# A two-layer decoder trunk on one core: matmul operands at the low end of SBUF, the softmax exchange on ScalarE, x loaded first, and a last FFN part of eight tiles

## The chip, the core and the metric

The kernel runs on one core of one Trainium2 chip. A core has TensorE (PE in the profile; its weight loads are shown apart as PEld), VectorE (DVE), ScalarE (ACT), GpSimd (POOL) and SyncE (SP), which here only starts transfers. SP, ACT and POOL each have a DMA queue. On-chip memory is SBUF, 128 partitions of 224 KB, and PSUM, where products are summed. The metric is the device time of one execution, in microseconds (us); lower is better. Before the change the median of 3 runs is 2288.46 us (2286.1 to 2291.06).

## The reference

One sequence of 512 tokens of width 1024, two layers. All in float32.

```python
def reference(x, ...):
    for l in range(2):
        mix = hybrid_mixer(x, rel_bias, w_in[l], b_in[l], w_attn_proj[l], w_ret_proj[l], w_out[l])
        x = layer_norm(ALPHA * x + mix, ln1_g[l], ln1_b[l])
        x = layer_norm(ALPHA * x + swiglu(x, w_ffn_gate[l], w_ffn_up[l], w_ffn_down[l]), ln2_g[l], ln2_b[l])
    return x

def hybrid_mixer(...):
    z = x @ w_in + b_in                    # split: q,k,v of attention (18 heads of 64); q,k (4 x 256), v, gate (4 x 512)
                                           # of retention; two gates of 1024
    # attention: 3 groups of 6 heads, (window, dilation) = (128,1), (512,4), (2048,16); T5 relative bias;
    # the groups' outputs are summed with weights softmax(log of their softmax denominators)
    # retention: sum over m <= n of gamma^(n-m) (rot(q_n) . rot(k_m)) v_m, group norm, times silu(gate)
    merged = sigmoid(gate_a) * (y_attn @ w_attn_proj) + sigmoid(gate_b) * (y_ret @ w_ret_proj)
    return merged @ w_out

def swiglu(x, w_gate, w_up, w_down):       # inner width 2816 = 22 tiles of 128
    return (silu(x @ w_gate) * (x @ w_up)) @ w_down
```

## The kernel before

Every large product is made of three: each float32 operand is split into a rounded high part (ACT, `CAST`) and the rest (DVE, `TENSOR_TENSOR`), and high by high, high by low and low by high are summed in PSUM. The helper `hilo` makes the two parts, `mm3` issues the three products, all at line L78. The split weights are `whi` and `wlo` (4 buffers each), the split x is `xh` and `xl`, all of x transposed. Weights come through 8 buffers of 4 KB a partition, named `raw`; SP loads most of them.

A layer runs in stages. First the attention's q and k of the first head pair for two groups (`wstat_halves`, in two halves of 256 tokens, since x arrives token tile by token tile), then of the third group (`wstat`: weights stationary, 512 tokens moving). Then v, in two steps, by a seven-product scheme (`tall`, `ORDER`) that saves one product in eight. It needs sums of weight blocks (`P1`, `P3`): SP loads one block into a `raw` buffer and POOL's queue adds the other to it by an accumulating DMA (`Right.load`, L315). It also needs sums of x blocks (`S1` to `S4`, in `xs`), made by `x_sums` from copies of x named `xc`. The biases of these columns are a row product of `bh` and `ones`.

The attention itself is no stage: its small steps (scores, transposes, products with v) stand in a queue `side`, and `tick`, called after each large product, takes steps from it at the rate that `pace` sets. `nothing` entries only space the steps. There are three head pairs `hp`; a pair's steps run beside the q and k products of the next pair. The first group works in token order, the two dilated groups in an order by residue of 4. So after a pair's scores, `swap` copies its maxima `nm` and sums `ls` into `pk` and brings them through DRAM (`exd`) into token order (`mb`); `weigh` computes the weights of both orders and sends the dilated one back through DRAM into `fa`; `scale` multiplies the outputs `y` by `fa` (L553), `place` transposes them into `yaT`. `swap` stands at the end of a pair's steps, the other four (`tail`) among those of the next pair. The biases of the scores come from `bias_vectors`: a table product (`hot`), then `bias_d`, then `bias_r`, a copy for each of 128 partitions, 2.7 MB, then `load_bias` (L745 to L747) reads slices of it.

After that come retention (`rotary`, `ret_values_gates`, `ret_scores`, `ret_outputs`, with operands `rot`, `vr` and `pj`), the gates (`ya` is the split `yaT`), the projection of retention into `m`, and w_out, whose second half has the tokens as the outer loop (`token_outer`): one token tile's 24 products end, then `residual` and `norm` run on DVE while PE goes on with the next tile. The FFN goes in parts of the 22 inner tiles, `FPARTS`; each part makes its tiles `ht` by gate and up products and then adds its down products to the residual. The last part's second half is again token-outer, and its `norm` ends the layer: in layer 0 the result is transposed into the next layer's `xh` and `xl` (`to_xT`), in layer 1 it is stored.

The order on each engine is set by the Tile framework's scheduler, which also places the waits. Tiles come from pools that open and close with the stages; a pool lies where the ones opened before it end, counted from the low end of SBUF.

Of the kernel before, what the change touches and what calls it, by code (L numbers as in the profile page):

```python
# [49 lines left out]
FPARTS = ((0, 8), (8, 16), (16, 22))  # L50
# [3 lines left out]
def hybrid_kernel(ctx, tc, x, rel_bias, w_in, b_in, w_attn_proj, w_ret_proj, w_out,  # L54
# [20 lines left out]
    dve.memset(mhalf, -0.5)  # L75

# [100 lines left out]
    def x_sums(cp):  # L177

        (a11, a12), (a21, a22) = cp
        t = {}  # L180

        def put(n, v):
            o_ = xs[:, SN.index(n)]
            hilo(v, o_[:, 0], o_[:, 1])

        def tt(o_, a, b, op):
            dve.tensor_tensor(out=o_, in0=a, in1=b, op=op)

        def s1():
            t["s"], t["v"] = view(raw("sch"), 4, 256), view(raw("sch"), 4, 256)  # L190
            tt(t["s"], a21, a22, ALU.subtract)
            put("S1", t["s"])

        def s2():
            tt(t["s"], t["s"], a11, ALU.subtract)
            put("S2", t["s"])

        def s4():
            tt(t["s"], t["s"], a12, ALU.add)
            put("S4", t["s"])  # L200

        def s3():
            tt(t["v"], a11, a21, ALU.subtract)
            put("S3", t["v"])

        return [s1, s2, s4, s3]


    def pair_units(w, c, c2=None):

        out_ = []
        for hf in range(2):
            ks = slice(4 * hf, 4 * hf + 4)
            if c2 is None:
                r = load(w[:, ks, c:c + 256], 4, 256)
            else:
                r = view(raw(), 4, 256)
                v = r.rearrange("p k (q c) -> p k q c", q=2)
                for q, cc in enumerate((c, c2)):
                    nc.sync.dma_start(v[:, :, q], w[:, ks, cc:cc + P])  # L220
            out_.append(unit(r))
        return out_
# [251 lines left out]
    def attention_pair(hp, qk, v, yp, bias, yaT):  # L474
# [48 lines left out]

        def swap():

            exd = drp.tile([S, 4], F32, tag="exd", name="exd", bufs=2)
            pk = sm.tile([P, NI, 4], F32, tag="pk", name="pk", bufs=2)
            pool.tensor_copy(pk[:, :, 0:2], nm[:, 1])
            pool.tensor_copy(pk[:, :, 2:4], ls[:, 1])
            pool.dma_start(exd.rearrange("(l r) c -> l r c", r=4), pk)  # L530
            pool.dma_start(mb, exd.rearrange("(i p) c -> p i c", p=P))

        def weigh():
            exd2 = drp.tile([S, 2], F32, tag="exd2", name="exd2", bufs=2)
# [12 lines left out]
            pool.dma_start(exd2.rearrange("(i p) c -> p i c", p=P), wb)  # L547
            pool.dma_start(fa[:, 1], exd2.rearrange("(l r) c -> l r c", r=4))
            dve.tensor_tensor(out=fa[:, 0], in0=ea[:, 0], in1=wa, op=ALU.mult)

# [26 lines left out]
        tail = [weigh, lambda: (scale(0), scale(1)), lambda: place(0), lambda: place(1)]  # L577
# [15 lines left out]
    def layer(ly, cp):  # L593
# [9 lines left out]
        yap = lay.enter_context(tc.tile_pool(name="yap", bufs=1))  # L603
        yaT = yap.tile([P, NG, S], F32, name="yaT")
        csp = lay.enter_context(tc.tile_pool(name="csp", bufs=1))
        opp = lay.enter_context(tc.tile_pool(name="opp", bufs=9))
# [52 lines left out]
        with tc.tile_pool(name="attn", bufs=1) as ap_, tc.tile_pool(name="attw", bufs=4) as aw:  # L659
# [5 lines left out]
            def qk_units(hp, g):  # L665
                c = g * GW + hp * P
                return pair_units(w_l, C_QA + c, C_KA + c)
# [9 lines left out]
            if ly == 0:  # L677
                x0 = [slot("x0", F32) for _ in range(NI)]
                cp = [[slot("xc", F32).rearrange("p a (b t) -> p (a b) t", b=2) for _ in range(2)] for _ in range(2)]
# [416 lines left out]
```

## Time and profile before

| | us |
|---|---|
| median of 3 runs | 2288.46 (2286.1 to 2291.06) |
| the profiled execution's own time | 2290.13 |
| its span, first to last instruction | 2288.1 |
| PE busy | 2246.7 (98%) |
| DVE busy | 1184.5 (52%) |
| ACT busy | 847.9 (37%) |
| POOL busy | 198.9 (9%) |
| mean granted clock of PE | 0.992 |

The profile gives, for one execution, each instruction's start and end, what it waited for, and the clock that PE was granted (1.00 is full speed). A table by stretch sums these over a part of the span; a timeline row gives start, length, engine, line, operation and tiles, and in brackets the wait ahead of it. In rows of the form `out<-in`, buffer numbers are left out.

### The profile page before, as it was taken

To read this page: it belongs to the slowest core of one execution; us is meant where nothing else is said; L and a number is where in the kernel's file an instruction comes from. 1 tells how busy PE (TensorE), PEld (TensorE's weight loads), DVE (VectorE), ACT (ScalarE), POOL (GpSimd) and SP (SyncE) were. 2 spreads that over 40 slices of the span, in tenths; PEclk is the share of its full clock that TensorE was granted. 3 is DMA by queue.
4 is the path that set the end of the run, shared out by engine and by line. 5 is a ranking of instruction groups with operands and counts; after the bars stand their busy time and mean duration, and the time that the engine had idled before them with its cause. 6 is when DMAs were issued, how large, how long until landed. Compare 5 with 4: busy or idle time off the path is not lost.

```text
span 2288.1 us, 27786 instructions
## 1 busy us (share of the span) xinstructions
PE 2246.7 (98%) x10890; PEld 1848.0 (81%) x10890; DVE 1184.5 (52%) x1793; ACT 847.9 (37%) x1359; POOL 198.9 (9%) x276
## 2 busy tenths in 40 slices
PE   8899999999999999999999999999999999999997
PEld 7877778878888888888889777788888888888886
DVE  5534577776335533333576446777753455333345
ACT  4444545545333132222235445445543232322230
POOL 1310011110000100000031111111000001000001
PEclk9999999999999999999999999999999999999999
DMA  6953265455565233333249332665454752233320
GB/s 168 246 146 84 63 175 134 123 140 152 176 225 184 64 110 94 92 102 101 71 124 252 92 85 65 158 172 134 127 163 144 247 166 65 94 100 101 93 74 37
DMA packets 253875, 294.24 MB, mean 129 GB/s; under 512 B 13981, under 2 KB 192497, under 8 KB 253616
## 3 DMA queue, kind: packets, MB, share of 16 engines
q1 hardware_dynamic: 212640, 234.20, 34.1%
q0 software_dynamic: 22032, 45.69, 8.9%
q10 hardware_dynamic: 19072, 12.59, 1.8%
q8 instruction: 85, 1.39, 0.3%
q14 instruction: 46, 0.38, 0.1%
HBM read 266.63 MB, written 28.53 MB: 129 GB/s over the span
## 4 chain that ended last, share of the span: by engine, by line
PE 76%; issue 18%; DMA 3%; DVE 2%; POOL 1%; ACT 0%; SPq 0%; POOLq 0%; DVEq 0%; ACTq 0%
PE ps L78 68%; PE px L78 6%; DMA raw<-in_w_in 1%; PE px L507 1%; PE px L829 1%; POOL ry L121 1%; DMA fa<-exd 0%; DMA x<-in_x 0%; DVE xtok L922 0%; PE px L166 0%; DMA v_d<-sn 0%; DMA exd<-pk 0%; DVE stats L933 0%; DMA exd<-wb 0%; PE px L558 0%
## 5 line engine op out<-in xcount | busy, mean ns | idle before, releaser
L78 PE MATMUL ps<-xh,whi 128*128 128x512 f32 (+1 forms) x1760 | 676.7, 386 | 3.0 <-ACT xh L89 3.0
L78 PE MATMUL ps<-xl,whi 128*128 128x512 f32 (+1 forms) x1760 | 661.6, 376 | 0.1
L78 PE MATMUL ps<-xh,wlo 128*128 128x512 f32 (+1 forms) x1760 | 661.4, 376 | 0.0
L90 DVE TENSOR_TENSOR wlo<-raw,whi 128x1024 fp32r<-128x1024 f32 (+1 forms) x274 | 332.9, 1216 | 555.9 <-ACT whi L89 555.1
L89 ACT CAST whi<-raw 128x1024 fp32r<-128x1024 f32 (+1 forms) x274 | 285.5, 1044 | 493.0 <-PE ps L78 421.9
L78 PEld LDWEIGHTS ps<-xh,whi 128*128 128x128 f32 x1760 | 332.7, 190 | 66.6 <-issue 6.4
L78 PEld LDWEIGHTS ps<-xh,wlo 128*128 128x128 f32 x1760 | 333.0, 189 | 60.3
L78 PEld LDWEIGHTS ps<-xl,whi 128*128 128x128 f32 x1760 | 333.9, 190 | 53.9 <-DVE xl L90 0.8
L78 PE MATMUL ps<-whi,xs 128*128 128x512 f32 (+1 forms) x768 | 224.4, 366 | 4.1 <-ACT whi L324 4.0
L330 DVE TENSOR_TENSOR wlo<-raw,whi 128x1024 fp32r<-128x1024 f32 (+1 forms) x168 | 178.7, 1065 | 91.6 <-ACT whi L324 91.0
L324 ACT CAST whi<-raw 128x1024 fp32r<-128x1024 f32 (+1 forms) x168 | 154.3, 925 | 126.4 <-PE ps L78 98.6
L78 PE MATMUL ps<-whi,ht 128*128 128x512 f32 x608 | 191.0, 393 | 0.0
L78 PEld LDWEIGHTS ps<-whi,xs 128*128 128x128 f32 x768 | 139.5, 190 | 28.8 <-ACT whi L324 6.6
L121 POOL TENSOR_TENSOR ry<-ve,mhalf 128x1 f32<-128x1 f32 x48 | 44.9, 936 | 1145.8 <-DVE ve L120 1145.8
L78 PE MATMUL ps<-wlo,xs 128*128 128x512 f32 (+1 forms) x384 | 139.5, 363 | 0.6 <-DVE wlo L330 0.6
L78 PEld LDWEIGHTS ps<-whi,ht 128*128 128x128 f32 x608 | 114.2, 188 | 28.4
L78 PE MATMUL ps<-wlo,ht 128*128 128x512 f32 x304 | 121.4, 399 | 0.0
L78 PE MATMUL ps<-whi,xh 128*128 128x512 f32 (+1 forms) x288 | 107.1, 372 | 3.6 <-DVE sn L434 3.6
L78 PE MATMUL ps<-whi,xl 128*128 128x512 f32 (+1 forms) x288 | 103.3, 359 | 0.0
L78 PE MATMUL ps<-wlo,xh 128*128 128x512 f32 (+1 forms) x288 | 103.2, 358 | 0.0
L315 POOL DMA_DIRECT2D raw<-in_w_in x48 | 59.3, 1263 | 279.0 <-DMA raw<-in_w_in 156.5
L78 PEld LDWEIGHTS ps<-wlo,xs 128*128 128x128 f32 x384 | 73.1, 190 | 10.3 <-DVE wlo L330 1.6
(172 smaller groups left out, 2526.9 us busy)
## 6 DMA issues: line engine op xcount, KB each, us to landing
raw<-in_w_in SPq DMA_DIRECT2D x144, 512.0 KB, 4.2
raw<-in_w_ffn_gate SPq DMA_DIRECT2D x44, 512.0 KB, 3.8
raw<-in_w_ffn_up SPq DMA_DIRECT2D x44, 512.0 KB, 3.8
raw<-in_w_ffn_down SPq DMA_DIRECT2D x44, 512.0 KB, 3.7
raw<-in_w_in SPq DMA_DIRECT2D x72, 256.0 KB, 4.8
raw<-in_w_in POOLq DMA_DIRECT2D x32, 512.0 KB, 7.5
raw<-in_w_ret_proj SPq DMA_DIRECT2D x32, 512.0 KB, 4.3
raw<-in_w_in SPq DMA_DIRECT2D x40, 288.0 KB, 4.8
```

The source lines that it names most:

```text
L78: pe.matmul(ps, lhsT=a, rhs=b, start=start, stop=stop, skip_group_check=True)
L89: act.copy(out=hi, in_=src)
L90: dve.tensor_tensor(out=lo, in0=src, in1=hi.bitcast(F32), op=ALU.subtract)
L121: pool.tensor_tensor(out=y, in0=ve, in1=mhalf, op=ALU.pow)
L315: pool.dma_start(r, self.src({"P1": "B12", "P3": "B22"}[n], u), accum_op=ALU.add)
L324: act.copy(out=h, in_=src)
L330: dve.tensor_tensor(out=l, in0=src, in1=h.bitcast(F32), op=ALU.subtract)
L507: pe.transpose(px[:, (2 + j) * P:(3 + j) * P], s[:, hh, j * P:(j + 1) * P], ident)
L829: pe.transpose(px[:, t * P:(t + 1) * P], ys[i][:, t * P:(t + 1) * P], ident)
```

## The change

It has these parts.

- **Pools.** `raw` and the small tiles `sm` are put at the high end of SBUF (`side="right"`), with `yaT`, cos and sin and the residual. The weight halves `whi`, `wlo` now follow x directly, and the operands of the stages (`opp`, `fo`, `mp`, `ret`, `attn`) follow those. The pools of the stages wait for earlier users tile by tile (`reuse_waits="tile"`) and not for the whole of a closed pool. The copies `xc` take four `raw` buffers.
- **Exchange.** The copies to `pk` and all four DMAs of the exchange move from POOL to ACT, and four tail steps become seven, each at its own place in `side`.
- **Start.** The identity goes to ACT's queue; x tiles 0 and 1 go ahead of all weights on SP, tiles 2 and 3 between the weight loads. The first units are split into their two column halves (`apart`), and `bias_vectors` runs within the first products.
- **x_sums** works in place, in another order of the four sums.
- **FPARTS** has its short part first: six, eight and eight tiles.

The number of products and of weight bytes is unchanged. Where the tiles lie, in KB of a partition as the two programs are built:

| tile | before | after |
|---|---|---|
| xh, xl, xs | 9 to 73 | 9 to 73 |
| raw | 73 to 105 | 188 to 220 |
| whi, wlo | 105 to 137 | 73 to 105 |
| qk, rot, vr, ya | 163 to 199 | 117 to 153 |
| ht | 177 to 221 | 117 to 161 |
| m | 177 to 209 | 117 to 149 |
| pj | 201 to 211 | 155 to 165 |

```diff
-FPARTS = ((0, 8), (8, 16), (16, 22))
+FPARTS = ((0, 6), (6, 14), (14, 22))
...
-    rawp = ctx.enter_context(tc.tile_pool(name="rawp", bufs=8))
     wp = ctx.enter_context(tc.tile_pool(name="wp", bufs=4))
     wk = ctx.enter_context(tc.tile_pool(name="wk", bufs=6))
-    sm = ctx.enter_context(tc.tile_pool(name="sm", bufs=4))
+    sm = ctx.enter_context(tc.tile_pool(name="sm", bufs=4, side="right"))
+    rawp = ctx.enter_context(tc.tile_pool(name="rawp", bufs=8, side="right"))
...
+    def stage(name, bufs=1, side="left"):
+        return tc.tile_pool(name=name, bufs=bufs, side=side, reuse_waits="tile")
...
+    def x_copies():
+        return [[view(raw("xc"), 4, 256) for _ in range(2)] for _ in range(2)]
...
+    def pair_units(w, c, c2=None, apart=False):
...
+            for hf, q in sorted(todo, key=lambda t: t[::-1]) if apart else todo:
+                nc.sync.dma_start(vs[hf][:, :, q * P:(q + 1) * P], w[:, 4 * hf:4 * hf + 4, (c, c2)[q]:(c, c2)[q] + P])
...
         def swap():
...
-            pool.tensor_copy(pk[:, :, 0:2], nm[:, 1])
-            pool.tensor_copy(pk[:, :, 2:4], ls[:, 1])
-            pool.dma_start(exd.rearrange("(l r) c -> l r c", r=4), pk)
-            pool.dma_start(mb, exd.rearrange("(i p) c -> p i c", p=P))
+            act.copy(out=pk[:, :, 0:2], in_=nm[:, 1])
+            act.copy(out=pk[:, :, 2:4], in_=ls[:, 1])
+            act.dma_start(exd.rearrange("(l r) c -> l r c", r=4), pk)
+
+        def swapped():
+            act.dma_start(mb, exd.rearrange("(i p) c -> p i c", p=P))
...
-            pool.dma_start(exd2.rearrange("(i p) c -> p i c", p=P), wb)
-            pool.dma_start(fa[:, 1], exd2.rearrange("(l r) c -> l r c", r=4))
+            act.dma_start(exd2.rearrange("(i p) c -> p i c", p=P), wb)
             dve.tensor_tensor(out=fa[:, 0], in0=ea[:, 0], in1=wa, op=ALU.mult)
+
+        def weighed():
+            act.dma_start(fa[:, 1], exd2.rearrange("(l r) c -> l r c", r=4))
...
-        tail = [weigh, lambda: (scale(0), scale(1)), lambda: place(0), lambda: place(1)]
+        tail = [swapped, weigh, weighed, lambda: scale(0), lambda: place(0), lambda: scale(1), lambda: place(1)]
...
-        yap = lay.enter_context(tc.tile_pool(name="yap", bufs=1))
+        yap = lay.enter_context(stage("yap", side="right"))
...
-        opp = lay.enter_context(tc.tile_pool(name="opp", bufs=9))
+        opp = lay.enter_context(stage("opp", 9))
...
-                nc.sync.dma_start(ident, c_id)
-                for hf in range(2):
-                    nc.sync.dma_start(x0[0][:, hf], x[:P, hf * S:(hf + 1) * S])
+                act.dma_start(ident, c_id)
...
+                load_x(0)
+                load_x(1)
...
-                us0 = []
-                for g in range(2):
-                    us0.append(qk_units(0, g))
-                    for i in ((1,), (2, 3))[g]:
-                        nc.sync.dma_start(x0[i], x[i * P:(i + 1) * P].rearrange("p (a b) -> p a b", a=2))
+                vecs = bias_vectors([aw.tile([P, S], F32, tag="bias", name="hot") for _ in range(NG)])
+                us0 = [qk_units(0, 0, True)]
+                load_x(2)
+                us0.append(qk_units(0, 1))
+                load_x(3)
+                cp = x_copies()
...
-                side.extend(ops[1] + [lambda l_=l_: bias_cols(l_) for l_ in range(DEPTH)] + ops[2] + ops[3])
+                side.extend(ops[1] + [lambda l_=l_: bias_cols(l_) for l_ in range(DEPTH)] + vecs[:3] + ops[2] + vecs[3:] + ops[3])
...
-            if ly == 0:
-                side.extend([nothing] + bias_vectors([aw.tile([P, S], F32, tag="bias", name="hot") for _ in range(NG)]))
-            pace(8 if ly else 16)
+            pace(8)
...
-                for at, f in zip((27, 25, 22, 15), reversed(tail)):
+                for at, f in zip((24, 22, 15, 14, 12, 8, 3), reversed(tail)):
                     ops.insert(at, f)
...
-        fo = fin.enter_context(tc.tile_pool(name="fo", bufs=11))
+        fo = fin.enter_context(stage("fo", 11))
...
-            if last and not final:
-                cp = [[fo.tile([P, 2, S], F32, tag="op", name="xc").rearrange("p a (b t) -> p (a b) t", b=2)
-                       for _ in range(2)] for _ in range(2)]
...
+                if tail and not final:
+                    cp.extend(x_copies())
```

How the order on the engines moves, at three places. SP, the start of the program, before:

```order
L686 DMA ident<-const_id 128x128
L688 DMA x_111<-in_x 128x512 x2
L220 DMA raw<-in_w_in 128x4x128 x4
L695 DMA x_112<-in_x 128x1024
L220 DMA raw<-in_w_in 128x4x128 x4
```

and after:

```order
L689 DMA x_108<-in_x 128x512 x2
L689 DMA x_109<-in_x 128x512 x2
L209 DMA raw<-in_w_in 128x4x128 x4
L689 DMA x_110<-in_x 128x512 x2
L209 DMA raw<-in_w_in 128x4x128 x4
```

The second tile of x has moved ahead of the first four weight loads. POOL's queue around the v products of layer 0, before (`bias_d` and `bias_r` are the bias vectors, L315 the accumulating weight loads, L745 to L747 the bias slices):

```order
L315 DMA raw<-in_w_in 128x2x288 x4
L463 DMA bias_d<-bv 6x383
L463 DMA bias_d<-bv 6x255 x2
L466 DMA bias_r<-bias_d 128x5358
L408 MEMSET rb 33x576
```

and after:

```order
L458 DMA bias_d<-bv 6x383
L458 DMA bias_d<-bv 6x255 x2
L461 DMA bias_r<-bias_d 128x5358
L403 MEMSET rb 33x576
```

The bias vectors now stand ahead of all accumulating loads (L310 in the new numbering), the first of which follows eight bias slices later. The exchange of the second head pair in layer 0, on POOL before (L315 are weight loads of the next stage):

```order
L528 COPY pk<-nm 128x4x2
L529 COPY pk<-ls 128x4x2
L530 DMA exd<-pk 128x16
L315 DMA raw<-in_w_in 128x2x512
L531 DMA mb<-exd 128x4x4
L547 DMA exd_2230<-wb 128x4x2
L548 DMA fa<-exd_2230 128x8
```

and on ACT after (L513 and L503 are copies of the attention's steps, L92 a weight cast):

```order
L525 COPY pk<-nm 128x4x2
L526 COPY pk<-ls 128x4x2
L527 DMA exd<-pk 128x16
L513 COPY y<-px 128x64 x2
L503 COPY sT<-px 128x256 x2
L530 DMA mb<-exd 128x4x4
L513 COPY y<-px 128x64
L539 ACTIVATE ea<-ea 128x16
L513 COPY y<-px 128x64
L545 DMA exd_1590<-wb 128x4x2
L503 COPY sT<-px 128x256 x2
L92 CAST whi<-raw 128x1024
L513 COPY y<-px 128x64 x2
L549 DMA fa<-exd_1590 128x8
```

On DVE after, the place where the result is used (the scores of the third pair are L492):

```order
L553 TENSOR_TENSOR y<-y,fa 128x512
L93 TENSOR_TENSOR wlo<-raw,whi 128x1024
L675 TENSOR_SCALAR qk<-ps,bT 128x512
L553 TENSOR_TENSOR y<-y,fa 128x512
L93 TENSOR_TENSOR wlo<-raw,whi 128x1024
L492 ISA s,nm<-px,bias 128x128
```

The exchange has left POOL and stands on ACT with two to four of ACT's rows between its steps; on DVE the row that waits for `fa` still stands ahead of the scores, as before.

More of the change, by code (lines that the diff above doesn't have):

```diff
@@ L214, in pair_units @@
             if c2 is None:
-                r = load(w[:, ks, c:c + 256], 4, 256)
+                vs.append(load(w[:, ks, c:c + 256], 4, 256))
             else:
[L217 to L221, printed above, removed]
+                vs.append(view(raw(), 4, 256))
+        if c2 is not None:
+            todo = [(hf, q) for hf in range(2) for q in range(2)]
+            for hf, q in sorted(todo, key=lambda t: t[::-1]) if apart else todo:
+                nc.sync.dma_start(vs[hf][:, :, q * P:(q + 1) * P], w[:, 4 * hf:4 * hf + 4, (c, c2)[q]:(c, c2)[q] + P])
+        if not apart:
+            return [unit(v) for v in vs]
+        out_ = [tuple(view(wp.tile([P, 1024], F32R, tag=t, name=t), 4, 256) for t in ("whi", "wlo")) for _ in vs]
+        for q in range(2):
+            for v, (h, l) in zip(vs, out_):
+                cs = slice(q * P, (q + 1) * P)
+                hilo(v[:, :, cs], h[:, :, cs], l[:, :, cs])
         return out_
@@ L777, in layer @@
                 pace(32)
[L778 removed]
+            n = [nothing]
+            side.extend(n * 3 + tail[:1] + n * 4 + tail[1:2] + n * 3 + tail[2:5] + n * 6 + tail[5:6] + n * 2 + tail[6:])
             pace(42)
```

50 lines of the change are left out of this document (18 added, 32 removed).

## The prediction

> **What bounds the kernel now.** I read the page first, for who is busy and whose chain ends last.
>
> ```profile
> span 2288.1 us, 27786 instructions
> PE 2246.7 (98%) x10890; PEld 1848.0 (81%) x10890; DVE 1184.5 (52%) x1793; ACT 847.9 (37%) x1359; POOL 198.9 (9%) x276
> PE 76%; issue 18%; DMA 3%; DVE 2%; POOL 1%; ACT 0%; SPq 0%; POOLq 0%; DVEq 0%; ACTq 0%
> ```
>
> TensorE (PE) is busy 98% of the span, and the chain that ends last is its products. So the time falls in two ways only: products that follow each other faster, or the 41 us (2288.1 − 2246.7) in which PE does nothing, with the slow clock after each pause. I therefore went on with tables by stretch, in which each row gives the stretch and its length, busy time and count of PE, weight loads, DVE, ACT and POOL, then granted clock and DMA share.
>
> **Pace and addresses.** Two stretches in which PE never pauses and the clock is full, the first in the FFN's gate/up products, the second in its down products:
>
> ```profile
> 920.00:1005.00 85.00, 85.00 (x377) 70.41 (x376) 28.20 (x31) 24.84 (x31) 0.00 (x0) 1.00 0.30 93
> 1007.50:1050.50 43.00, 43.00 (x186) 34.62 (x185) 14.27 (x15) 7.93 (x9) 0.00 (x0) 1.00 0.36 103
> ```
>
> A product's record lasts 0.39 us (groups below), so a stretch counts all that start in its length plus 0.39: 85.39/377 = 0.2265 us from start to start, against 43.39/186 = 0.2333. Same shape, same type, full clock in both. The groups, with count, busy time and mean ns of one, tell the operands apart:
>
> ```profile
> L78 PE MATMUL ps<-xl,whi 128*128 128x512 f32 x446 | 173.7, 390 | 0.0
> L78 PE MATMUL ps<-whi,ht 128*128 128x512 f32 x608 | 191.0, 393 | 0.0
> L78 PE MATMUL ps<-wlo,ht 128*128 128x512 f32 x304 | 121.4, 399 | 0.0
> L78 PE MATMUL ps<-xs,m 128*128 128x512 f32 x192 | 46.6, 398 | 0.0
> L78 PE MATMUL ps<-whi,m 128*128 128x512 f32 x128 | 40.3, 393 | 0.0
> L78 PE MATMUL px<-vr,pj 128*128 128x512 f32 x240 | 60.6, 393 | 0.0
> ```
>
> Those that read ht, m, vr or pj last 393 to 399 ns against 390. What these tiles share is the place: in the allocation of before they lie above 163 KB of a partition, x and the weight halves below 138 KB. I take the 6.8 ns (0.2333 − 0.2265) for every product with ht or m: 1056 with ht (608 + 304 here, 144 as xs,ht in two last parts; the tail's 72 are shown below) and 384 with m (192, 128 and by the code 64 with wlo), so 1440 × 6.8 ns = 9.8 us. The 144 with ya (by the code) at the same price are 1.0; the 240 of retention at 4 ns are 1.0. Were all brought below the border, 11.8 us. But the border lies somewhere between 138 and 163 KB. In the allocation of after, 48% of these 2016 products' operands (the full-width ones and the narrower retention ones) lie wholly below 138, 3% above 163, the rest between. Both ends: 5.7 (nothing gained between) and 11.8. Taken 8.5, the middle, since no row lies between.
>
> The Trainium skill, "TensorE: Matmul & The Clock Gate", section "Back-to-back issue gap", gives the warm gap by the free size alone, N/2.4 + 2.5 ns, and "SBUF — State Buffer", section "Who interferes with whom", says that PE never waits on anyone; by these the term is zero. The two stretches differ by 3% at one N, so the trace does not agree, though no run here shows that the address is the reason. This is the first rival below.
>
> **Start.** The first token tile of x stands first on SP, the second behind four weight loads.
>
> ```profile
> 4.26 9.60 DMA x<-in_x
> 13.90 1.97 PE L166 MATMUL px<-ident,x 128*128 128x128 f32 x8 [6.13 <-DMA x<-in_x]
> 0.00:15.69 15.69, 8.08 (x22) 4.46 (x22) 4.65 (x11) 5.23 (x7) 7.12 (x17) 0.82 0.92 262
> 15.69:21.00 5.31, 5.31 (x28) 5.31 (x28) 4.04 (x6) 4.42 (x7) 0.02 (x1) 0.56 1.11 342
> ```
>
> Its load takes 9.60 us from the issue at 4.26, PE waits 6.13 for it, the first weight product starts at 15.69, and the clock is 0.56 for the next 5.31 us, which costs up to 0.44 × 5.31 = 2.3. Now both x tiles go ahead of the weights and the identity leaves SP for ACT's queue. But at a DMA share of 0.92 the bytes are the limit: the same 2 MB (two x tiles, four weight quarters) must land before the first product of both halves, so x earlier means weights later: one x tile is 0.5 MB, at 262 GB/s (last column) 2.0 us. Ends: 4 gained (6.13 of wait less those 2.0) and 4 lost (the 2.0, and 2 more as the transposes of x tiles 2 and 3 and three small table products now come in a bunch; eight transposes took 1.97 above). Taken 2, near the clock's 2.3.
>
> **v projection of layer 0.**
>
> ```profile
> 54.90:108.40 53.50, 47.48 (x297) 42.12 (x296) 28.64 (x46) 20.12 (x37) 18.46 (x27) 0.94 0.86 230
> 1203.10:1247.50 44.40, 44.40 (x305) 41.75 (x304) 29.05 (x47) 24.41 (x43) 5.21 (x5) 1.00 0.97 253
> POOL bias L745 <- DMA bias_r<-bias_d: 8.6, 1, 8.6
> 77.90 0.57 POOL L745 DMA_DIRECT2D bias<-bias_r  x1 [8.60 <-DMA bias_r<-bias_d]
> 94.25 1.20 POOL L315 DMA_DIRECT2D raw<-in_w_in  x1 [5.40 <-DMA raw<-in_w_in]
> ```
>
> The first row is layer 0, the second the same products in layer 1, without a pause. Layer 0 loses 53.50 − 47.48 = 6.0 idle and 0.06 × 53.5 = 3.2 of clock, 9.2 together. POOL stands 8.6 us before the bias loads (L745), until 77.90, and what is queued behind are the accumulating loads (L315) of the second half's weights, the last at 94.25. The change makes the bias vectors in the first products (three small products, three copies, four DMAs, the same count, moved some 40 us ahead), so on POOL the broadcast is long down when the accumulating loads come. Against it: the copies of x now hold four of the eight weight buffers until x_sums is done, and the loads of P3 reuse buffers late. Ends 5 (a wait of 5.40 less some, or the clock as it is, stays) and 9.2. Taken 9, since layer 1 runs the same products without loss.
>
> **Softmax exchange.** For each of three head pairs, the maxima and sums of one token order are brought into the other through DRAM (pk, exd, mb), and the factors go back the same way (wb, exd, fa).
>
> ```profile
> DVE y L553 <- DMA fa<-exd: 30.6, 6, 6.2
> 204.14 0.58 POOL L530 DMA_DIRECT2D exd<-pk  x1 [0.32 <-POOL pk L529]
> 209.45 0.80 POOL L531 DMA_DIRECT2D mb<-exd  x1 [1.50 <-DMA exd<-pk]
> 215.62 0.76 POOL L547 DMA_DIRECT2D exd<-wb  x1 [5.37 <-DVE fa L549]
> 220.15 0.55 POOL L548 DMA_DIRECT2D fa<-exd  x1 [3.77 <-DMA exd<-wb]
> 224.93 0.69 DVE L553 TENSOR_TENSOR y<-y,fa 128x512 f32<-128x512 f32 x1 [6.16 <-DMA fa<-exd]
> 226.67 0.28 DVE L497 CUSTOM_DVE_ANT_0 s<-px,bias 128x128 f32<-128x128 f32 x1
> 227.54 0.86 PE L507 MATMUL px<-ident,s 128*128 128x128 f32 x2 [5.16 <-ACT s L499]
> 160.00:220.00 60.00, 59.94 (x338) 47.47 (x336) 26.51 (x70) 26.62 (x80) 9.23 (x14) 1.00 0.37 85
> 220.00:232.00 12.00, 6.84 (x29) 4.71 (x26) 4.35 (x12) 2.01 (x9) 0.55 (x1) 0.72 0.31 87
> 1345.00:1357.00 12.00, 7.60 (x32) 5.30 (x30) 4.35 (x12) 2.50 (x10) 0.55 (x1) 0.77 0.33 88
> ```
>
> DVE waits 6.16 us for fa at L553; the next pair's scores (L497) queue behind it, and PE, whose transposes need them, stands 5.16. Priced in records: 60.00/338 = 0.1775 us each undisturbed, so 29 are 5.1 us of work and 12.00 − 5.1 = 6.9 are lost; in layer 1, 32 are 5.7, 6.3 lost. Together 13.2; the other four of six waits cost PE little.
>
> The change gives ACT two copies and four DMAs per pair instead of POOL, and posts the steps three to eight ticks apart. On DVE the row that waits for fa still stands ahead of the next scores, so the gain is whatever fa lands sooner.
>
> ```profile
> v<-v_d SPq DMA_DIRECT2D x6, 64.0 KB, 1.9
> exd<-pk POOLq DMA_DIRECT2D x3, 8.0 KB, 2.5
> fa<-exd POOLq DMA_DIRECT2D x3, 4.0 KB, 4.4
> ```
>
> On POOL a 4 KB transfer takes 4.4 us from issue to landing, on SP 64 KB take 1.9. From 204.14 to fa's landing (224.9) there are four such DMAs; the last two alone (215.62 to 224.9 = 9.3) at 1.9 plus 1 of issue each are some 6, so fa lands 3 us earlier, and the first round trip 2 more: about 220, by an estimate, just when scores would start (226.67 − 6.16 = 220.5). Ends: 0 (fa as late as now) and 13.2. Taken 10.5, four fifths, as the estimate falls at the edge. ACT now waits for each round trip; that cover is ACT's 37%, and what it costs if gone is the rival below.
>
> The Trainium skill, "SBUF — State Buffer", box in "SBUF: two separate sides", says a DMA from POOL's queue can starve for descriptors while VectorE holds the shared port, and one from ACT or SP runs at full speed. By it the whole 13.2 would be had; the 4.4 against 1.9 us agree with it without proving the port.
>
> **Last part of eight tiles.**
>
> ```profile
> 774.90:797.40 22.50, 22.29 (x159) 20.47 (x157) 14.46 (x26) 4.13 (x8) 4.09 (x4) 1.00 0.13 47
> 1147.40:1169.50 22.10, 18.74 (x142) 17.24 (x140) 13.22 (x26) 7.34 (x14) 4.70 (x5) 1.00 0.18 72
> 2259.39 16.96 PE L78 MATMUL ps<-xs,ht 128*128 128x512 f32 x72
> 2267.93 1.42 DVE L922 SCALAR_TENSOR_TENSOR xtok<-xtok,ry,lnb 128x512 f32<-128x512 f32 x2
> 2283.33 1.41 DVE L922 SCALAR_TENSOR_TENSOR xtok<-xtok,ry,lnb 128x512 f32<-128x512 f32 x2
> ```
>
> In the last down products each token has 72/4 = 18 products, 16.96/4 = 4.24 us; the first token's normalisation ends at 2267.93 + 1.42 = 2269.35, the last's at 2284.74, so one per (2284.74 − 2269.35)/3 = 5.13 us: DVE falls behind and ends 8.4 us after PE (2276.35). With 24 products a token PE takes 24 × 0.2333 = 5.6 us and DVE keeps up: the tail becomes one chain, 5.5 us (PE gives the first token at 2263.6, 2269.35 is 5.7 after), so 2.8 less. The boundary between the layers has the same six tiles: 22.10 − 18.74 = 3.4 idle, while w_out's, which has eight, idles 0.2; 3.2 less. Sum 6.0, ends 4 and 8. The number of products is unchanged.
>
> Pool closings that wait by tile instead of by pool let some tiles be written earlier. Of PE's 41.4 idle us I have placed 7.6 before the first product (15.69 − 8.08), 6.0, 5.2, 4.4, 3.4 and 8.4, 35.0; of the other 6.4 at most a third may be such waits. Ends 0 and 2, taken 0, as these pools close under running products.
>
> **Sum.** 8.5 + 2 + 9 + 10.5 + 6 = 36. The profiled run took 2290.1 (span 2288.1 and 2.0 around it); 2290.1 − 36 = 2254.1, and the median of the runs is 1.7 below this run: 2252.
>
> **Rivals.** (1) The address does nothing: ht and m are slow for another reason. Then 2252 + 8.5 = 2261; against it, the six groups share nothing else. 0.16. (2) The exchange stall stays, as L553 still stands before the scores and fa is as late: 2252 + 10.5 = 2263; 0.11. (3) The v projection waits on, now for buffers held by the copies of x: 2252 + 9 = 2261; 0.08. (4) The other side: ACT, waiting for the exchange's round trips (2.5 + 4.4 us a pair, the exd rows above, if as slow as on POOL), holds up the weight casts queued behind. Six pairs × 6.9 = 41.4, times 6.9/6.16 = 1.12 for the clock: 46 us lost, nothing gained there; 2252 + 10.5 + 46 = 2309. It decides when more than 25.5 + 4.6 = 30 us of the 46 reach PE. Against it: four weight buffers let the casts run ahead, and SP's row has 1.9 us for more bytes. 0.05. (5) Layout, exchange and start all fail: near 2280 to 2290, 0.04.
>
> **How the numbers follow.** The forecast holds 0.56 at 2252, its own range 2242 to 2264. Three rivals lie at 2261 to 2263, inside a range of 2240 (all upper ends: 11.8 + 4 + 9.2 + 13.2 + 8 + 2 = 48) to 2272 (two of the rivals at once, near 2272); with the forecast's edges 0.2 at most are outside. Below 0.2% (4.6 us, about what a measurement can tell from no change): faster 0.92, same 0.03 from (5), slower 0.05 from (4).
>
> **What would show it.** ht and m products starting 227 ns apart; no pause of PE at the first scores of the third pair in either layer, fa landing before 221; layer 0's v projection near 45 us; PE's end to span's end below 6; the second x tile landed by 8 us. I am wrong first of all if the groups still read 393 and 399, or if PE waits for ACT's casts within the attention.

## The result, and the profile after

The changed kernel takes 2251.22 us, the median of 4 runs (2249.55 to 2254.58), against 2287.93 for the kernel before (4 runs, 2286.1 to 2291.06): a ratio of 0.984, 95% interval 0.9823 to 0.9857, or 36.7 us less. The prediction said 2252, 36 less. Its profiled execution took 2250.18 with a span of 2248.4; the profiled one of before was 2.2 us above its own median, so the two traces differ by more, 39.7 us of span.

From the page of the changed kernel:

```profile
span 2248.4 us, 27714 instructions
PE 2223.7 (99%) x10890; PEld 1841.0 (82%) x10890; DVE 1184.3 (53%) x1795; ACT 844.7 (38%) x1373; POOL 180.8 (8%) x240
PE 74%; issue 16%; DMA 4%; DVE 3%; POOL 1%; ACT 1%; POOLq 0%; DVEq 0%; ACTq 0%
```

PE is still the bound. Its idle time fell from 41.4 to 24.7 us, and its busy time by 23.0 at an unchanged 10890 products: part of that is pace, part the clock. The pace, in the groups of products (line, operands, count, busy us, mean ns of one):

```profile
L81 PE MATMUL ps<-xl,whi 128*128 128x512 f32 x1504 | 586.5, 390 | 0.0
L81 PE MATMUL ps<-whi,ht 128*128 128x512 f32 x576 | 178.3, 389 | 0.0
L81 PE MATMUL ps<-wlo,ht 128*128 128x512 f32 x288 | 112.0, 389 | 0.0
L81 PE MATMUL px<-vr,pj 128*128 128x512 f32 x240 | 59.6, 389 | 0.0
```

The 393 and 399 of before are gone in these groups, also for operands that lie up to 161 KB. (One group still reads 393, xs with m, which read 398 before; by their starts its products are as fast as the rest, 227.3 ns apart in place of 233.3.) The stretches, with columns as in the prediction: the start, the v projection of layer 0 (from the first product with xs to the first scores), the attention of layers 0 and 1 (from the first scores to the first product of retention; the row of layer 0 ends 0.25 us short of it, so it stands for 172.3), and the end of layer 0.

```profile
0.00:14.50 14.50, 6.95 (x22) 3.62 (x22) 4.98 (x12) 5.65 (x10) 4.59 (x12) 0.92 0.90 265
63.70:110.00 46.30, 45.90 (x314) 42.87 (x313) 30.36 (x46) 23.31 (x40) 7.88 (x10) 1.00 0.98 244
110.00:282.00 172.00, 168.84 (x931) 132.70 (x931) 84.23 (x195) 82.03 (x241) 12.56 (x17) 0.99 0.40 99
1223.10:1391.40 168.30, 167.63 (x932) 131.80 (x932) 84.74 (x195) 82.08 (x241) 12.96 (x18) 1.00 0.40 102
1118.00:1142.00 24.00, 23.03 (x144) 20.38 (x143) 22.09 (x39) 8.77 (x13) 6.30 (x6) 1.00 0.34 113
```

The attention stretches of before, between the same two products:

```profile
119.70:295.30 175.60, 170.38 (x933) 133.25 (x933) 84.10 (x195) 82.79 (x235) 21.74 (x36) 0.98 0.37 94
1245.40:1421.00 175.60, 171.15 (x933) 134.06 (x933) 84.33 (x195) 83.08 (x235) 21.72 (x36) 0.98 0.38 96
```

So the v projection lost its pauses (0.4 us idle, clock 1.00), the attention became 3.3 us shorter in layer 0 and 7.3 in layer 1, and the end of layer 0 idles 1.0. At the end of the program PE stops at 2217.73 + 21.92 = 2239.65, 8.75 us ahead of the span's end, where it was 11.75 (2276.35 to 2288.1):

```profile
2217.73 21.92 PE L81 MATMUL ps<-xs,ht 128*128 128x512 f32 x96
```

### The profile page after: what moved, and what is told of

It reads as the page before. It is cut to its first block, busy times and chain, and to the rows that moved or that the text cites. A ratio compares the mean times of both kernels' runs of the same rounds, so it can differ in the third digit from the quotient of the medians.

```text
span 2248.4 us, 27714 instructions
## 1 busy us (share of the span) xinstructions
PE 2223.7 (99%) x10890; PEld 1841.0 (82%) x10890; DVE 1184.3 (53%) x1795; ACT 844.7 (38%) x1373; POOL 180.8 (8%) x240
## 4 chain that ended last, share of the span: by engine, by line
PE 74%; issue 16%; DMA 4%; DVE 3%; POOL 1%; ACT 1%; POOLq 0%; DVEq 0%; ACTq 0%
PE ps L81 66%; PE px L81 6%; DMA raw<-in_w_in 2%; PE px L502 1%; POOL ry L124 1%; PE px L833 1%; DMA exd<-wb 1%; DMA fa<-exd 1%; DVE wlo L325 1%; DVE xtok L926 1%; DMA rb<-in_b_in 0%; DMA exd<-pk 0%; DMA mb<-exd 0%; DVE stats L937 0%; PE px L169 0%
## 5 line engine op out<-in xcount | busy, mean ns | idle before, releaser
L93 DVE TENSOR_TENSOR wlo<-raw,whi 128x1024 fp32r<-128x1024 f32 (+2 forms) x274 | 330.8, 1208 | 528.2 <-ACT whi L92 527.7
L92 ACT CAST whi<-raw 128x1024 fp32r<-128x1024 f32 (+2 forms) x274 | 282.8, 1035 | 462.9 <-PE ps L81 399.6
L325 DVE TENSOR_TENSOR wlo<-raw,whi 128x1024 fp32r<-128x1024 f32 (+1 forms) x168 | 178.7, 1064 | 81.1 <-ACT whi L319 80.3
L319 ACT CAST whi<-raw 128x1024 fp32r<-128x1024 f32 (+1 forms) x168 | 154.2, 923 | 118.8 <-PE ps L81 92.6
L81 PE MATMUL ps<-whi,ht 128*128 128x512 f32 x576 | 178.3, 389 | 0.0
L81 PEld LDWEIGHTS ps<-whi,ht 128*128 128x128 f32 x576 | 108.1, 188 | 22.4
L81 PE MATMUL ps<-wlo,ht 128*128 128x512 f32 x288 | 112.0, 389 | 0.0
L310 POOL DMA_DIRECT2D raw<-in_w_in x48 | 59.2, 1234 | 293.0 <-DMA raw<-in_w_in 204.0
```

Of the source, the lines that this page charges most:

```text
L81: pe.matmul(ps, lhsT=a, rhs=b, start=start, stop=stop, skip_group_check=True)
L92: act.copy(out=hi, in_=src)
L93: dve.tensor_tensor(out=lo, in0=src, in1=hi.bitcast(F32), op=ALU.subtract)
L310: pool.dma_start(r, self.src({"P1": "B12", "P3": "B22"}[n], u), accum_op=ALU.add)
L319: act.copy(out=h, in_=src)
L325: dve.tensor_tensor(out=l, in0=src, in1=h.bitcast(F32), op=ALU.subtract)
```

## The experiments

All times are medians beside runs of the kernel before in the same series (2287.56, 2288.21 and 2287.59 in the three series). "The changed kernel" is the 2251.22 above.

| run | what differs | us | ratio to before, interval |
|---|---|---|---|
| b_layout | before, with the pools laid out as after | 2275.43 | 0.9945, 0.9932 to 0.9957 |
| a_low_raw | changed, raw and sm back at the low end | 2262.10 | 0.9888, 0.9874 to 0.9901 |
| b_pad | before, and 96 unused bytes | 2276.94 | 0.9949, 0.9936 to 0.9961 |
| a_fparts_old | changed, parts 8, 8, 6 | 2263.71 | 0.9895, 0.9882 to 0.9909 |
| a_vecs_late | changed, bias vectors late | 2258.82 | 0.9867, 0.9853 to 0.9880 |
| a_ex_pool | changed, exchange on POOL | 2257.89 | 0.9867, 0.9852 to 0.9882 |
| a_ex_oldplaces | changed, exchange on ACT, old places | 2251.25 | 0.9840, 0.9825 to 0.9855 |
| a_ex_sp | changed, exchange on SP | 2242.74 | 0.9802, 0.9788 to 0.9815 |
| a_start | changed, x cast first | 2246.39 | 0.9824, 0.9811 to 0.9838 |
| a_start_sp | the last two together | 2242.20 | 0.9801, 0.9788 to 0.9815 |

### The layout: is it the address?

The kernel before with the new layout only:

```diff
-    rawp = ctx.enter_context(tc.tile_pool(name="rawp", bufs=8))
-    sm = ctx.enter_context(tc.tile_pool(name="sm", bufs=4))
+    sm = ctx.enter_context(tc.tile_pool(name="sm", bufs=4, side="right"))
+    rawp = ctx.enter_context(tc.tile_pool(name="rawp", bufs=8, side="right"))
...
+    # yap, csp and fin also with side="right"
```

> The kernel before with its pools laid out as after (raw, sm, yaT, cos and sin, residual at the high end), and the same order on PE, DVE and ACT. Theory A (address): products with ht, m, ya, vr, pj start 227 ns apart, 11.4 us faster, near 2276.5. Theory B (not the address): no change, 2288.

2275.43, 12.1 less: the layout is worth that by itself. The other way round, in the changed kernel, with no instruction moved:

```diff
+    rawp = ctx.enter_context(tc.tile_pool(name="rawp", bufs=8))
     wp = ctx.enter_context(tc.tile_pool(name="wp", bufs=4))
...
-    sm = ctx.enter_context(tc.tile_pool(name="sm", bufs=4, side="right"))
-    rawp = ctx.enter_context(tc.tile_pool(name="rawp", bufs=8, side="right"))
+    sm = ctx.enter_context(tc.tile_pool(name="sm", bufs=4))
```

> The changed kernel with raw and sm back ahead of the weight halves at the low end; no instruction moves on any engine, the weight halves lie at 105 to 137 KB and ht at 153 to 197. Theory A (address): the ht tiles that lie above 163 KB are slow again, eight of eleven, so 8 to 11 us slower than the changed kernel, near 2260. Theory B: 2251, as the changed kernel.

2262.10, 10.9 more, as the theory of the address said. But the groups in its trace say that the theory is wrong:

```profile
L81 PE MATMUL ps<-whi,ht 128*128 128x512 f32 x576 | 181.0, 393 | 0.0
L81 PE MATMUL ps<-wlo,ht 128*128 128x512 f32 x288 | 114.9, 399 | 0.0
```

These are the means of before exactly, though here ht begins at 153 KB, and in the changed kernel it reached 161 at 389. Taken tile by tile, from the start of a product of whi with ht to the next start, the ht tile at 152 to 156 KB goes at 231.3 ns and the others at 231.2 to 231.3 (behind a product of wlo it is 237.5 for all). A border that moves with the kernel is none. The run that has the pairs of addresses alone:

> A kernel of its own, nothing of the reference's work but the copy of x to the output: 13 tiles of 16 KB a partition, named a to m in order of address (8 to 205 KB), and for each pair (moving operand from one, stationary from another) 18 products of 512 columns, each with the other of two stationary blocks. Theory A (pace depends on where the operands lie): pairs with both operands below 138 KB follow each other every 226.8 ns, pairs with the stationary operand above 163 KB every 231 to 238, as in the profile before; the table shows the border. Theory B (ht, m, ya and pj were slow for what they are, or for the DMA traffic of raw beside them): all 169 pairs at 226.8, within 1 ns.

All 169 pairs but the first, which has the cold clock, start 226.6 to 226.7 ns apart. Three of its timeline rows (18 products each, moving operand first): 40 KB with 204, 120 with 172, a pair like wlo and ht before, and 200 with 188:

```profile
160.41 4.24 PE L33 MATMUL px<-atc,atm 128*128 128x512 f32 x18
417.45 4.24 PE L33 MATMUL px<-ath,atk 128*128 128x512 f32 x18
686.73 4.24 PE L33 MATMUL px<-atm,atl 128*128 128x512 f32 x18
```

The address theory fell here, and with it the first step of the prediction. What the layouts also change is the start of a tile modulo a small power of two: `sm` is 3.6 KB long, no multiple of 512 bytes, and what was allocated behind it (qk, rot, vr, ya, ht, m, pj) was shifted against x and the weight halves. Modulo 512 bytes those started at 320 in before and a_low_raw, and at 160 in the changed kernel and b_layout; x and the weight halves start at 160 in all. Sorted by this over five traces (before, the changed kernel, b_layout, a_low_raw and a_fparts_old), some 34000 products with both operands at 160 start 227.4 ns apart, some 2800 with the stationary operand at 320 and some 280 with the moving one there 233.3 and 233.7, and 576 with both at 320 some 231. The smallest edit that tells it from the address:

```diff
+    ctx.enter_context(tc.tile_pool(name="padp", bufs=1)).tile([P, 24], F32, name="pad")
     sm = ctx.enter_context(tc.tile_pool(name="sm", bufs=4))
```

> The kernel before with one unused tile of 96 bytes a partition ahead of the small tiles, nothing else; the order on all engines is the same and the operands stay at the high end (ht at 177 to 221 KB), but start at 32 modulo 64 bytes like x and the weight halves, where they started at 0. Theory C or D (the residue): 12 us faster, near 2275.5, as the layout alone gave. Theory A (low end): 2287.5, no change.

2276.94: 11.3 us for 96 bytes that nothing reads, with ht still at 177 to 221 KB. Its tiles start at 416 modulo 512 now, which is 160 modulo 256, as x and the weight halves do. The groups of that run:

```profile
L78 PE MATMUL ps<-whi,ht 128*128 128x512 f32 x608 | 188.0, 389 | 0.0
L78 PE MATMUL ps<-wlo,ht 128*128 128x512 f32 x304 | 118.3, 389 | 0.0
```

That the residue alone does it, without the kernel's other traffic, is shown by the last run of this set:

> A kernel of its own, nothing of the reference's work but the copy of x: 16 moving tiles (ma to mp) and 16 stationary tiles (sa to sp), whose starts lie 32 bytes further each, modulo 512 bytes; for each of the 256 pairs 18 products of 512 columns. All tiles lie below 70 KB. Theory C (pace depends on the operand's start modulo 64 bytes, as the four groups of residues in the traces of before, after and the layout runs suggest): 226.7 ns where both residues are 32 modulo 64, about 233 where one is 0 and the other 32, about 231 where both are 0. Theory D (the residue matters only beside the kernel's other traffic): 226.7 for all pairs, as the pairs of addresses gave.

Five of its rows. Tile mb starts at 32 modulo 512, mk at 320; the stationary tiles sh, si, sj and sl at 224, 256, 288 and 352, sc at 64:

```profile
103.61 4.29 PE L36 MATMUL px<-mb,sh 128*128 128x512 f32 x18
107.74 4.37 PE L36 MATMUL px<-mb,si 128*128 128x512 f32 x18
111.94 4.28 PE L36 MATMUL px<-mb,sj 128*128 128x512 f32 x18
120.25 4.36 PE L36 MATMUL px<-mb,sl 128*128 128x512 f32 x18
684.36 4.25 PE L36 MATMUL px<-mk,sc 128*128 128x512 f32 x18
```

17 steps and one record of 0.39 us make a row, so mb with si goes at (4.37 − 0.39)/17 = 0.234 us, mb with sj at 0.229 and mk with sc at 0.227. From the starts of the 255 pairs with a warm clock (second to last start of a row), by the difference of the two residues (stationary less moving, modulo 256 bytes), the mean of some 32 pairs each in ns; within a group they differ by 1.5 at most:

| 0 | 32 | 64 | 96 | 128 | 160 | 192 | 224 |
|---|---|---|---|---|---|---|---|
| 228.0 | 233.2 | 233.3 | 233.9 | 232.1 | 233.5 | 229.0 | 233.3 |

The kernel before had a difference of 160 with ht and m and of 96 with ya: 233.3 and 233.7 by their starts, as the table. In 16 more pairs of this run the moving operand starts 4 to 24 bytes off a multiple of 32, and their products start 230 to 240 ns apart.

Theory C as it was written does not hold to the letter (a difference of 64, with both residues equal modulo 64, is as slow as 32). Nor is the difference all: among the pairs with a difference of 0, mk with sc is one of only two at 226.6, the others take some 228. And the 288 products of retention with 512 columns, whose operands have one residue in every trace, go at some 231 in the kernel before, where both start at 320, but at 226.7 in b_pad, where both start at 416. What is shown: where the two operands start costs up to 3% of the pace at starts that are multiples of 32; most of that goes with their difference modulo 256 bytes, and at equal residues the pace in this run is full or within 1% of it (226.6 to 228.1). Why, and what the absolute start adds, the runs don't tell. The Trainium skill, "SBUF — State Buffer", section "Who interferes with whom", gives PE two independent read ports and says that it never waits on anyone. From 20 to 1140 us of this run DVE, ACT and POOL did nothing, so no other engine is in question: the 3% goes with PE's own operands, and the measurement decides.

### The exchange: the queue or the places?

The four DMAs and two copies back on POOL, the new places kept:

```diff
-            act.copy(out=pk[:, :, 0:2], in_=nm[:, 1])
-            act.copy(out=pk[:, :, 2:4], in_=ls[:, 1])
-            act.dma_start(exd.rearrange("(l r) c -> l r c", r=4), pk)
+            pool.tensor_copy(pk[:, :, 0:2], nm[:, 1])
+            pool.tensor_copy(pk[:, :, 2:4], ls[:, 1])
+            pool.dma_start(exd.rearrange("(l r) c -> l r c", r=4), pk)
...
+            # the other three DMAs also by pool
```

> The changed kernel with the exchange's copies and four DMAs back on POOL, the seven tail steps where they are now. Theory (the queue brings the gain): fa late again, PE waits about 5 us at the third pair's first scores in both layers, 10 us slower, near 2261. Rival (the places of the steps bring it, ACT's queue is no faster): fa as now, and ACT no longer stands before the copies of sT, 2248 to 2252.

And the queue kept, the steps back at their old places (`swap` with `swapped`, `weigh` with `weighed`, both `scale` together):

```diff
-                for at, f in zip((24, 22, 15, 14, 12, 8, 3), reversed(tail)):
+                for at, f in zip((27, 25, 22, 15), reversed(tail)):
```

> The changed kernel with the exchange on ACT, but in two steps at the places that they had before. Theory (the queue and the places each bring a part; on POOL the new places left 6 us in each layer): ACT waits for each round trip in one piece, 4 to 8 us slower than the changed kernel, near 2257. Rival (ACT's queue alone brings all): 2251.

2257.89 and 2251.25. By the attention stretches the same: both layers together take 351.2 us before, 348.1 with the new places on POOL, 341.1 on ACT at the old places, 340.6 in the changed kernel. Other traces with the same exchange show how far such a sum varies: b_layout and b_pad, on POOL at the old places, take 348.9 and 347.3; a_low_raw, a_fparts_old, a_vecs_late and a_start, on ACT at the new places, 338.5 to 341.6. So the step from POOL to ACT brings some 8 us (6 to 13 by the extremes), and the spaced places nothing that can be told on either queue. The second theory, that both bring a part, fell.

What the queue changes is not mainly the transfer. The medians from issue to landing in layer 0's attention, for the last two DMAs, on POOL (a_ex_pool), on ACT (the changed kernel) and on SP (below):

```profile
exd<-wb POOLq DMA_DIRECT2D x3, 4.0 KB, 4.7
fa<-exd POOLq DMA_DIRECT2D x3, 4.0 KB, 4.5
...
exd<-wb ACTq DMA_DIRECT2D x3, 4.0 KB, 4.8
fa<-exd ACTq DMA_DIRECT2D x3, 4.0 KB, 3.0
...
exd<-wb SPq DMA_DIRECT2D x3, 4.0 KB, 4.3
fa<-exd SPq DMA_DIRECT2D x3, 4.0 KB, 2.3
```

The write of wb takes 4.3 to 4.8 on every queue (4.0 to 4.6 in layer 1). fa comes 1.5 to 2.2 sooner off POOL here, but in layer 1 it takes 4.0 on POOL and on ACT alike, and 1.8 on SP. The copies to pk, 1.4 us on POOL, are 0.4 on ACT. From the copy to pk to the use of fa the second pair's exchange took 22.1 and 21.4 us before (layers 0 and 1), 19.9 and 20.8 in a_ex_pool, 18.3 and 16.0 in the changed kernel. Most of this came ahead of wb's issue: 12.8 and 13.5 us from the copy to there before, 10.9 and 7.9 in the changed kernel. From there to the use of fa it was 9.3 and 7.9 before, 7.5 and 8.1 after, so in layer 1 the last two DMAs gained nothing.

But ACT pays for it. Its timeline in layer 0, and what PE waited for, in the changed kernel:

```profile
198.97 0.38 ACTq L530 DMA_DIRECT2D mb<-exd  x1
204.21 0.21 ACT L539 ACTIVATE ea<-ea 128x16 f32<-128x16 f32 x1 [3.81 <-DVE ea L538]
205.37 0.38 ACTq L545 DMA_DIRECT2D exd<-wb  x1
205.79 0.65 ACT L503 COPY sT<-px 128x256 f32<-128x256 f32 x2 [1.27 <-DVE fa L546]
...
206.21 1.43 PE L81 MATMUL px<-v,sT 128*128 128x64 f32 x8 [3.04 <-ACT sT L503]
```

ACT stands for mb's landing, then for wb, and the copy of sT that PE needs is queued behind: 3.04 us of PE, with a clock of 0.73 from 205 to 209 us. This is the mechanism of the prediction's fourth rival, with copies in place of weight casts, in one place of six. So the DMAs went to a queue with no compute behind it:

```diff
-            act.dma_start(exd.rearrange("(l r) c -> l r c", r=4), pk)
+            nc.sync.dma_start(exd.rearrange("(l r) c -> l r c", r=4), pk)
...
+            # the other three DMAs also by nc.sync
```

> The changed kernel with the exchange's four DMAs on SP's queue and the two copies still on ACT; the same order on PE, DVE and POOL. Theory (ACT, standing for the round trips, holds up the copies of sT: the 3.0 us wait of PE in layer 0): that wait goes, fa lands as soon as now, 3 to 4 us faster than the changed kernel, near 2247.5. Rival (SP's loads of v and weights, queued behind the exchange's waits, come late): 2 to 6 us slower, 2253 to 2257.

2242.74, 8.5 us less than the changed kernel, and the intervals of the two ratios don't meet. Its longest wait of this kind:

```profile
PE px L81 <- ACT sT L503: 0.9, 1, 0.9
```

The attention takes 168.1 and 166.9 us, 5.6 less than in the changed kernel (334.9 in both layers again in a_start_sp, which also has SP), and the second pair's exchange 15.7 and 14.2. SP's own loads behind the waits cost nothing that shows. The gain is twice what was expected, and what is over 5.6 is not shown to be SP's. Behind the attention this trace is 2.5 us shorter than the changed kernel's, and a short wait of PE in retention for a sum on DVE (1.0 us in layer 0) is gone; but a_ex_oldplaces, on ACT, has the same 2.5. Ahead of the first scores it is 2.3 longer. Why stays open.

### The v projection

```diff
-                vecs = bias_vectors([...])
...
             side.extend(x_sums(cp))
+            if ly == 0:
+                side.extend([nothing] + bias_vectors([...]))
```

> The changed kernel with the bias vectors made where they were before, after the first products. Theory: POOL holds up the accumulating loads again, PE idles 6 us in layer 0's v projection at a slower clock, 9 us slower, near 2260. Rival (x first and the copies of x in raw buffers changed that stage): within 3 us of 2251.

2258.82, 7.6 more, and the stretch is that of before, with its pauses and its clock:

```profile
63.40:118.50 55.10, 48.92 (x314) 44.90 (x313) 30.17 (x45) 23.25 (x40) 14.43 (x22) 0.94 0.95 269
```

55.1 us against 46.3 in the changed kernel: the early bias vectors bring 8.8 in this stretch, the theory. All traces agree: from the first product with xs to the first scores, the four with late vectors (before, b_layout, b_pad and this one) take 54.8 to 55.9 us, the eight with early ones 45.3 to 48.4.

### The last part of eight tiles

```diff
-FPARTS = ((0, 6), (6, 14), (14, 22))
+FPARTS = ((0, 8), (8, 16), (16, 22))
```

> The changed kernel with the FFN parts of before (8, 8, 6 tiles). Theory: DVE falls behind again in both last parts, 2.6 us of idle at the layer boundary and 3.3 at the end, near 2257. Rival: the boundary was short for another reason (copies of x in other buffers), then only the end's 3, near 2254.

2263.71, 12.5 more, twice what was expected. The stretch that follows the end of layer 0 in this run (the same window is shown above for the changed kernel), and one wait:

```profile
1118.00:1142.00 24.00, 17.79 (x85) 14.62 (x84) 21.40 (x42) 7.92 (x12) 7.76 (x7) 0.86 0.18 72
PE ps L81 <- ACT whi L92: 4.0, 1, 4.0
```

6.2 us idle and a clock of 0.86, where before the change the same six tiles cost 3.4. In the new kernel the casts of the next layer's weights stand on ACT among the copies of x (xc), which wait for DVE, and xc holds raw buffers; with six tiles DVE is late and the next layer's weights with it (the waits show the first part; that the raw buffers are the link, no run tests). So the old parts cost more beside the other edits than they did before: from layer 0's first product of retention to layer 1's first scores, b_layout, with the old parts and the new layout, takes 944.8 us, this run 949.4 and the changed kernel 940.8. The parts of the change are not a plain sum.

### The start

The casts of x tiles 0 and 1 ahead of the first weight casts (in `pair_units`, a call back before the halves are split):

```diff
+        apart()
         out_ = [tuple(view(wp.tile([P, 1024], F32R, tag=t, name=t), 4, 256) for t in ("whi", "wlo")) for _ in vs]
...
-                us0 = [qk_units(0, 0, True)]
+                us0 = [qk_units(0, 0, lambda: [f() for f in ops[0] + ops[1]])]
```

> The changed kernel with the casts of x tiles 0 and 1 ahead of the first weight casts on ACT (the transposes of tile 1 run with those of tile 0, not from the side queue). Theory (the first product waits for the last x cast, which stands behind four weight casts that wait for their loads): first weight product near 12.4 in place of 14.5, 2 us faster, near 2249. Rival (the weights' bytes are the limit): first product earlier, but PE then waits for each weight quarter, 2251, no change.

The first weight product comes at 12.2 us in place of 14.5, but in this trace the stretch up to the first scores gives nearly all of it back:

```profile
53.50:109.70 56.20, 54.32 (x363) 49.92 (x362) 34.85 (x52) 26.65 (x46) 9.94 (x11) 1.00 0.88 223
56.00:110.00 54.00, 53.60 (x365) 49.86 (x364) 34.96 (x53) 26.89 (x46) 10.39 (x12) 1.00 0.97 240
```

The first row is this run, the second the changed kernel, both from the first bias row to the first scores: 56.2 against 54.0, 0.3 us left. But this trace, of 2251.36, is the slowest of its four runs, the others being 2245.45 to 2246.73, and the first scores come at 108.2 to 112.3 us in the six traces with the changed kernel's start. So 0.3 can't be told from a gain of 2, and neither theory is shown. The median, 2246.39, is 4.8 below the changed kernel's, with intervals that meet; where it comes from stays open.

> Both of the last edits together, the exchange's DMAs on SP and x's casts first: if both theories hold, 2245 to 2246; if the two rivals hold, 2253 to 2257.

2242.20, 0.5 less than with SP alone, so x's casts bring nothing that can be told there. a_ex_sp and a_start_sp are the fastest versions, 45 us below the kernel before.

## Why the prediction was right, point by point

The time was right and one of its reasons wrong.

| step | predicted | measured | by |
|---|---|---|---|
| layout | 8.5 | 11.4 | starts of the products in both traces; 12.1 in b_layout |
| start | 2 | 0.8 | first product with xs, 64.5 to 63.7; not clear of the spread between traces |
| v projection | 9 | 8.9 | stretch, 55.2 to 46.3; 7.6 in a_vecs_late |
| exchange | 10.5 | 10.6 | attention stretches, 351.2 to 340.6; some 8 over all traces |
| last part, boundary | 3.2 | 2.4 | idle, 3.4 to 1.0 |
| last part, tail | 2.8 | 3.0 | PE's end to the span's end, 11.75 to 8.75 |

These make 37.1 of the 39.7 us between the two spans; the rest lies in small pieces that were not followed.

**Layout.** The step that failed is "What these tiles share is the place", and what it rests on, "the border lies somewhere between 138 and 163 KB". The slow groups shared their place and also their residue, and the prediction looked only at the first: its argument against the first rival, that "the six groups share nothing else", was wrong. Its full price, 11.8, was right, since the new layout gave every tile the residue of x; the 8.5 was too low because half of the gain was doubted for a border that isn't there. The first rival had the cause right ("ht and m are slow for another reason") and the time wrong: the address does nothing, and the layout still brought it all.

**Start.** The term was over-sized: 0.8 in place of 2, and traces with one and the same start differ by more (62.7 to 64.2 us with the new start, 62.9 to 64.5 with the old). x landed early, as it said, but the first product then waited 6.07 us for a cast of x on ACT, which stood behind weight casts that waited for their loads. That the bytes are the limit, which the step named and still priced at a gain, fits this; a_start does not settle it.

**v projection.** Right in size and cause; the third rival (buffers held by the copies of x) did not come.

**Exchange.** The size was right, and in part by luck. The price of 1.9 us for each of the last two DMAs, from SP's larger transfer, did not hold: wb's write takes 4.8 on ACT, and from wb's issue to fa's use it was 7.5 and 8.1 us, not 6, against 9.3 and 7.9. What made up for it came ahead of wb's issue, 1.9 us in layer 0 and 5.6 in layer 1, where the step had 2; the copies to pk are 1 us of it. Its sign, fa before 221 us, was met (used at 212.8) because the attention began 9.7 us sooner: counted from the first scores, fa was used after 105.2 us before and 102.8 after, and the forecast 220 stood for 100.3. The other sign held: PE's wait at the scores fell from 9.6 us to 0.6. The layers differ, 3.3 and 7.3, for ACT's wait of 3.04 in layer 0, the mechanism of the fourth rival at a fifteenth of its price. The sentence on the Trainium skill's box ("SBUF — State Buffer", "SBUF: two separate sides") is borne out in part: off POOL's queue fa came 1.5 to 2.2 us sooner in layer 0, in layer 1 on SP alone; exd<-wb came hardly sooner, and not the whole 13.2 was had.

**Last part.** Right, 5.4 for 6.0; that the old parts would cost 12.5 in the new kernel was not foreseen. The last normalisation ends 5.6 us behind PE, as the working gave (5.5). The sign "PE's end to span's end below 6" was not met, 8.75, since the span also holds the last store, which the sign left out.

## What to carry to other kernels

When one group of products is slower than another of the same shape, compare the starts of their two operands modulo 256 bytes too, before blaming the place: a small odd-sized pool ahead of them can shift a whole stage by some bytes, and a pad of 96 bytes brought 11 us here. A chain of small transfers with waits between belongs on a queue with no compute behind it: POOL, ACT and SP gave 2257.9, 2251.2 and 2242.7 for the same work. And undo the parts of a change one at a time: the right total hid a wrong cause, and one part was worth twice as much beside the others as had been reckoned for it. Where one stretch decides, compare it over all traces that share its code: here the same instructions differed by 3 to 4 us from trace to trace.

## What the runs showed of the hardware that was not expected

- Products of 512 columns start 226.6 ns apart wherever their operands lie (169 pairs, 8 to 205 KB, all starts at one residue), but 232 to 234 apart for six of eight differences of the operands' starts modulo 256 bytes, with no other engine at work.
- The write of 4 KB in small pieces (exd<-wb) takes 4.0 to 4.8 us from issue to landing on POOL's, ACT's and SP's queue alike (medians of three, both layers).
